# h for the gate turned in blocks of 32 and moved through memory, and the gate computed token tile by token tile behind the whole projection

## The chip, the cores and the metric

The kernel runs on one core of a Trainium2 chip. The time is that of one execution on the device, in microseconds (us). The engines are PE (matrix products and transposes), DVE (elementwise), ACT (elementwise with functions and scales), POOL and SP, which here issues the transfers (SPq in the profile is its queue).

## The reference

Two layers over 256 tokens of width 1024. Each layer has a half-step feed-forward, a token mixing of two attention groups, a second half-step feed-forward and a per-layer embedding; a final normalisation ends it. The change concerns the last step of a layer, and the feed-forward only in how it hands h on.

```python
def rms_norm(x, g):
    y = x * rsqrt(mean(x * x, axis=-1) + EPS)
    return y * g

def hybrid_layer(h, p_i, ...):
    h = h + 0.5 * swiglu(rms_norm(h, ffn1_norm), ...)
    ...                                   # token mixing, added to h
    h = h + 0.5 * swiglu(rms_norm(h, ffn2_norm), ...)
    gate = sigmoid(rms_norm(h, ple_norm) @ w_ple_gate)    # 1024 x 1024
    h = h + gate * (p_i @ w_ple_proj)                     # p_i: 256 x 256
    return h
```

## The kernel before

The tokens are two tiles of 128 (`t` = 0, 1), each on 128 partitions; h stays on chip as `h[:, t, 0:1024]`, and columns are worked in two halves (`f` or `n` = 0, 1) of 512. Products are made to float32 accuracy from two parts of each operand, a high one and the rest: `mm3` is three matmuls (L265 to L267) of 0.23 us each for 512 columns, "a product" below. All weights stream in once, in pieces of 128x1024 (512 KB) that are numbered in the order of use: SP issues the load of `raw` (L157, 7 buffers), ACT copies the high part `wh` (L161), DVE subtracts to get the low part `wl` (L162); eight buffers hold the parts. The gate's weights in layer 0 are pieces 200 to 207 (200 to 203 the first column half), in layer 1 pieces 403 to 410; the two pieces before them are the projection's.

A product needs its left operand turned, with the inner dimension on partitions. `turn_h` (L379) turns a half row of h: four PE transposes of 128x128 (L385) into a bank of PSUM `xt`, four copies on ACT that scale by the norm's gain (L390, `xf`, tag `w2`, two buffers), a copy for the high part on ACT (L392), a subtraction for the low part on DVE (L393). The row's own scale (one over its root mean square) is applied later, as the scale of the sigmoid.

Work that has to be late in an engine's order is put off by a list: `soon(us, f)` puts f on it, and each product adds its modelled length (0.68 for 512 columns) to a count of PE time; what is due then is written out. `flush` writes out everything that is left. Instructions of one engine run in the order in which they are written, apart from small moves by a scheduler; waits are set from data and from buffers.

`lagging` (L423) runs the last products of a feed-forward, with tile 1 three chunks behind tile 0; with the last chunk of a tile comes `residual` (L412), which adds to h and puts `turn_h` on the list for both halves. Then `ple` (L1079) runs column half by column half: for each half four products of the projection (`pv`), then for tile 0 and for tile 1 eight products of the gate (`e`), the sigmoid on ACT (L1109, `se`), two operations on DVE (L1111 `me`, L1112 `h`), the sum of squares of the new h (ACT L354, `junk_ple`), and in layer 0 `turn_h` on the list for the next feed-forward (`xt_e`, `xf_e`, `xe0h`).

Elsewhere (`add` of the class `Gates`, L511) some tiles are already turned without PE: DVE turns blocks of 32x32 in place (L549), SP stores the tile to memory (L551, `m_`) and loads it back in four strided pieces (L556, `ft_`).

Of the kernel before, what the change touches and what calls it, by code (L numbers as in the profile page):

```python
# [17 lines left out]
P = 128  # L18
T = 256
DM = 1024  # L20
# [25 lines left out]
def turned_order(n):  # L46


    import numpy as np

    return np.arange(n).reshape(n // P, 4, 32).transpose(1, 0, 2).reshape(-1)
# [20 lines left out]
def trunk(ctx: ExitStack, tc: tile.TileContext, xT, xr, pT, w, gains, fgain, consts, out):  # L72
# [12 lines left out]
    def bank(name):  # L85
        return ps.tile([P, 512], F32, tag="A", name=name)
# [46 lines left out]
    at = [0]  # L133
    ids = itertools.count()
    newest_load, newest_wh, newest_wl = [None], [None], [None]
    fence = [None, None]

    class Unit:
# [10 lines left out]
        def load(self, q, i):  # L149
            name = f"{self.u}_{q}_{i}_{next(ids)}"  # L150
            if q not in self.parts:
                self.parts[q] = tuple(w_p.tile([P, PIECE], F32R, tag=f"w{e}", name=f"w{e}{name}") for e in "hl")
            n = PIECE // self.sub
            wh, wl = (t[:, i * n : (i + 1) * n] for t in self.parts[q])
            r = raw_p.tile([P, PIECE], F32, tag="raw", name=f"raw{name}")[:, :n]
            a = q * PIECE + i * n
            newest_load[0] = nc.sync.dma_start(r, w[self.u, :, a : a + n])  # L157
            for c in range(self.cut):
                a = slice(c * n // self.cut, (c + 1) * n // self.cut)
                two = (  # L160
                    nc.scalar.activation(wh[:, a], r[:, a], AF.Copy),  # L161
                    nc.vector.tensor_tensor(wl[:, a], r[:, a], wh[:, a].bitcast(F32), ALU.subtract),  # L162
                )
                newest_wh[0], newest_wl[0] = two
                for i, f in zip(two, fence):
                    if f is not None:
                        after(i, f)
# [77 lines left out]
    def soon(us, f):  # L245
        due.append((pe[0] + us, len(due), f))
# [8 lines left out]
    def flush():  # L255
        while due:
            i = min(due)
            due.remove(i)
            i[2]()
# [3 lines left out]
    def mm3(o, a, b, start, stop, **kw):  # L263
        (ah, al), (bh, bl) = a, b
        nc.tensor.matmul(o, ah, bh, start=start, stop=False, **kw)  # L265
        nc.tensor.matmul(o, ah, bl, start=False, stop=False, **kw)  # L266
        newest_mm[0] = nc.tensor.matmul(o, al, bh, start=False, stop=stop, **kw)  # L267
        tick(0.36 if o.shape[-1] <= T else 0.68)

    def both(x, *ix):  # L270
        return tuple(t[ix] for t in x)

    def tok(x, k, t):

        return both(x, slice(None), k, slice(t * P, (t + 1) * P))
# [9 lines left out]
    def wide(us):  # L285

        return lambda k: us[k // 4].at(k % 4, 0, 512)
# [13 lines left out]
    def half(f):  # L301
        return slice(f * 512, (f + 1) * 512)
# [76 lines left out]
    def turn_h(x, t, n, gcol, name):  # L379

        a = bank(f"xt{t}{n}_{name}")
        behind = newest_mm[0]
        for j in range(4):
            c = 4 * n + j
            after(nc.tensor.transpose(a[:, j * P : (j + 1) * P], h[:, t, c * P : (c + 1) * P], ident), behind)  # L385

        f = flat("w2", f"xf{t}{n}_{name}").rearrange("p (a b) -> p a b", a=4)
        for j in range(4):
            c = gcol + 4 * n + j
            nc.scalar.activation(f[:, j], a[:, j * P : (j + 1) * P], AF.Copy, scale=g_sb[:, c : c + 1])  # L390
        xh, xl = both(x, slice(None), slice(4 * n, 4 * n + 4), slice(t * P, (t + 1) * P))
        nc.scalar.activation(xh, f, AF.Copy)  # L392
        nc.vector.tensor_tensor(xl, f, xh.bitcast(F32), ALU.subtract)  # L393

    def column(r, name):

        d = wt("w1", f"col_{name}")
        nc.vector.tensor_tensor(d[:, :, :P], r.rearrange("p (a b) -> p a b", a=2), ident.unsqueeze(1).to_broadcast([P, 2, P]), ALU.mult)
        c = tp.tile([P, 2], F32, tag="col", name=f"c_{name}")
        nc.vector.reduce_sum(c, d[:, :, :P], axis=AX.X)  # L400
        return c
# [7 lines left out]
    def four(name):  # L409
        return [[bank(f"{name}{t}{n}") for n in range(2)] for t in range(2)]  # L410

    def residual(x, n, d, t, scale, tag, gcol, wait=(1.2, 1.9)):  # L412

        for f in range(2):
            c = half(f)
            done = nc.vector.scalar_tensor_tensor(h[:, t, c], d[t][f], scale, h[:, t, c], op0=ALU.mult, op1=ALU.add)
            soon(wait[f], lambda f=f: turn_h(x, t, f, gcol, tag))
        for f in range(2):
            n.add(t, half(f))
        n.done(t)  # L420
        return done

    def lagging(chunks, d, x, scale, tag, gcol, lag, first=True):  # L423

        nx, nn = new_x(f"x_{tag}"), Norm(tag)
        N = len(chunks)
        for i in range(N + lag):
            for t, c in ((0, i), (1, i - lag)):
                if 0 <= c < N:
                    u, j, k = chunks[c]  # L430
                    down_mm(d, u, j, x(k), x.at(k), t, first and c == 0, c == N - 1)
                    if c == N - 1:
                        done = residual(nx, nn, d, t, scale, tag, gcol)
                        if t == 0 and fence[1] is not None:

                            fence[1] = done
        return nx, nn
# [130 lines left out]
    def ffn(x, n, tag, gcol, between=None, feed=None):  # L568
# [163 lines left out]
        nc.vector.tensor_tensor(b, p[5], v, ALU.subtract)  # L732
        to_h(1, 0, v)
        fence[1] = to_h(1, 1, b)
        return lagging(rest, d, gates, 0.5, tag, gcol, 3, False)

    def mix(x, n, L, g0):
        st = {}
# [340 lines left out]
    def ple(x, n, xp, L, gcol):  # L1079
        last = gcol is None  # L1080
        if last:
            nx = None
            fg = f_p.tile([P, DM], F32, tag="f4h", name="fg")
            nc.sync.dma_start(fg, fgain)
            hg = x_p.tile([P, 2, DM], F32, tag="xh", name="hg")
        else:
            nx = new_x(f"xe{L}")
        nn = Norm(f"ple{L}")
        up = Unit(2)
        for f in range(2):  # L1090
            c = half(f)
            wf = wide([Unit(4) for _ in range(2)])
            v = [bank(f"pv{L}{f}{t}") for t in range(2)]
            for k in range(2):
                for t in range(2):
                    mm3(v[t], tok(xp, k, t), up.at(k, c.start, c.stop), k == 0, k == 1, skip_group_check=True)
            for t in range(2):

                step = 256 if last and f == t == 1 else 512
                for a in range(0, 512, step):  # L1100
                    p = slice(a, a + step)
                    hc = h[:, t, c.start + a : c.start + a + step]
                    e = bank(f"e{L}{f}{t}{a}")[:, :step]
                    for k in range(KC):
                        mm3(e, tok(x, k, t), both(wf(k), slice(None), p), k == 0, k == KC - 1, skip_group_check=True)
                    if f == t == 0:
                        flush()
                    s = flat("w0", f"se{L}{f}{t}{a}")[:, :step]
                    sig = nc.scalar.activation(s, e, AF.Sigmoid, scale=n.col(t))  # L1109
                    m = flat("w1", f"me{L}{f}{t}{a}")[:, :step]  # L1110
                    nc.vector.tensor_tensor(m, v[t][:, p], s, ALU.mult)  # L1111
                    nc.vector.tensor_tensor(hc, m, hc, ALU.add)  # L1112
                    nn.add(t, slice(c.start + a, c.start + a + step))
                    if last:
                        nc.vector.tensor_tensor(hg[:, t, c.start + a : c.start + a + step], hc, fg[:, c.start + a : c.start + a + step], ALU.mult)
                    else:
                        soon(4.4 if f == 0 else 2.8, lambda t=t, f=f: turn_h(nx, t, f, gcol, f"e{L}"))
                if f:
                    nn.done(t)
                    if last:  # L1120
                        leave(hg, nn, t)
        if not last:
            table_after(SILU, sig)
        return nx, nn
# [38 lines left out]
def _weights(i):  # L1163
# [9 lines left out]
    for L in range(DEPTH):  # L1173

        def wide(w, m):

            units.extend(cols(w[k : k + 512], m) for k in range(0, DM, 512))
# [49 lines left out]
        ffn("ffn2")  # L1227
        units.append(cols(i["w_ple_proj"][L], ar(DM)))
        for m in range(0, DM, 512):
            wide(i["w_ple_gate"][L], ar(m, m + 512))  # L1230
    return np.stack(units)


def _gains(i):
    import numpy as np

    names = ("ffn1_norm", "mix_norm", "q_lat_norm", "kv_lat_norm", "sb_out_norm", "mla_out_norm", "ffn2_norm", "ple_norm")
    g = [i[n][L].reshape(-1, P) for L in range(DEPTH) for n in names] + [i["final_norm"].reshape(-1, P)]
    return np.ascontiguousarray(np.concatenate(g).T)


# [45 lines left out]
```

## Time and profile before

| what | us |
| --- | --- |
| median of 3 runs | 986.97 (986.43 to 987.26) |
| the profiled execution, its own time | 986.99 |
| its span, first to last instruction | 985.2 |
| PE busy in it | 973.5 (99%) |
| DVE busy | 841.8 (85%) |
| ACT busy | 644.2 (65%) |
| raw weight loads: 338 of 512 KB, from issue to landing, median | 5.5 |

The profile is of one execution. "Busy" counts the time in which an engine runs an instruction. PE rows overlap: a matmul of 0.39 us follows the one before after 0.23. A row of a timeline has the start, the length, the engine, the line and operation, output and inputs, and how many instructions it stands for; in brackets stand the idle time before it and what ended that. The embedding of layer 0 begins with the residual of tile 0 at 458.05, that of layer 1 with the one at 942.89.

### The profile page before, as it was taken

The page shows a single profiled execution, that of the slowest core. Times are in us where ns is not written, and L with a number is a line of the kernel's source. Part 1 is how long each engine was busy: PE and PEld are TensorE (multiplying, and loading weights), DVE is VectorE, ACT ScalarE, POOL GpSimd, SP SyncE. Part 2 cuts the span into 40 slices and gives each one's busy share as a digit, 9 for nine tenths or more (in the row PEclk, how much of TensorE's full clock was granted, in tenths as well). Part 3 has the DMA queues.
Part 4 walks back from the last instruction along what each step waited for, and adds up shares of the span by engine and source line. Part 5 has one row for each costly group of instructions (what it writes and reads, how often), then busy time and mean ns, then how long its engine had stood idle before and what let it go on. Part 6 is the DMA issues. An engine that isn't in the chain of part 4 may idle for free.

```text
span 985.2 us, 13903 instructions
## 1 busy us (share of the span) xinstructions
PE 973.5 (99%) x4880; PEld 823.8 (84%) x4880; DVE 841.8 (85%) x1025; ACT 644.2 (65%) x958; POOL 55.5 (6%) x59
## 2 busy tenths in 40 slices
PE   9999999999999999999999999999999999999997
PEld 7888888899978888888888888889998888888886
DVE  5799899965689998999799989998656999989994
ACT  6756566856587566657776655667757866656663
POOL 0000000200120000001110000003000200000020
PEclk9999999999999999999999999999999999999999
DMA  8948766763074788666648686658602667876651
GB/s 295 365 153 296 244 199 214 255 231 113 11 246 156 250 263 303 177 229 219 230 134 286 229 275 212 215 210 298 206 32 71 229 199 253 294 228 202 222 173 44
DMA packets 85174, 208.39 MB, mean 212 GB/s; under 512 B 13680, under 2 KB 33264, under 8 KB 85104
## 3 DMA queue, kind: packets, MB, share of 16 engines
q1 hardware_dynamic: 84672, 206.93, 62.9%
q8 instruction: 38, 0.62, 0.3%
q10 hardware_dynamic: 432, 0.57, 0.2%
q14 instruction: 32, 0.26, 0.1%
HBM read 195.94 MB, written 11.53 MB: 211 GB/s over the span
## 4 chain that ended last, share of the span: by engine, by line
PE 93%; DVE 3%; ACT 1%; issue 1%; DMA 1%; POOL 0%; POOLq 0%; SPq 0%; DVEq 0%; ACTq 0%
PE p_b L265 4%; PE p_b L267 4%; PE p_b L266 3%; PE g_a L265 3%; PE g_a L267 3%; PE g_a L266 3%; PE g_b L267 3%; PE g_b L266 3%; PE g_b L265 3%; PE p_a L266 3%; PE p_a L267 3%; PE p_a L265 3%; PE d_a L266 3%; PE d_b L265 3%; PE d_a L267 3%; PE d_b L267 3%
## 5 line engine op out<-in xcount | busy, mean ns | idle before, releaser
L162 DVE TENSOR_TENSOR wl<-raw,wh 128x1024 fp32r<-128x1024 f32 (+1 forms) x278 | 321.8, 1190 | 63.3 <-ACT wh L161 60.6
L161 ACT ACTIVATE wh<-raw 128x1024 fp32r<-128x1024 f32 (+1 forms) x278 | 281.6, 1038 | 100.1 <-DMA raw<-in_w 19.1
L202 ACT ACTIVATE wh<-raw 128x1024 fp32r<-128x1024 f32 x133 | 139.8, 1062 | 112.7 <-DVE raw L197 63.1
L203 DVE TENSOR_TENSOR wl<-raw,wh 128x1024 fp32r<-128x1024 f32 x133 | 161.2, 1221 | 10.3 <-ACT wh L202 8.5
L197 DVE TENSOR_TENSOR raw<-raw,raw 128x1024 f32<-128x1024 f32 x76 | 92.6, 1222 | 1.3 <-DMA raw<-in_w 0.8
L265 PE MATMUL d_a<-wh,fh_a 128*128 128x512 f32 x108 | 42.4, 392 | 0.0
L265 PE MATMUL d_b<-wh,fh_b 128*128 128x512 f32 x108 | 42.4, 392 | 0.0
L267 PE MATMUL d_a<-wh,fl_a 128*128 128x512 f32 x108 | 42.1, 389 | 0.0
L267 PE MATMUL d_b<-wh,fl_b 128*128 128x512 f32 x108 | 42.1, 389 | 0.0
L266 PE MATMUL d_b<-wl,fh_b 128*128 128x512 f32 x108 | 42.0, 389 | 0.0
L266 PE MATMUL d_a<-wl,fh_a 128*128 128x512 f32 x108 | 42.0, 389 | 0.0
L265 PE MATMUL g_a<-wh,x0h 128*128 128x512 f32 x80 | 31.3, 393 | 0.7 <-ACT x0h L314 0.7
L267 PE MATMUL g_a<-wh,x0l 128*128 128x512 f32 x80 | 31.0, 389 | 0.0
L266 PE MATMUL g_a<-wl,x0h 128*128 128x512 f32 x80 | 31.0, 389 | 0.0
L265 PE MATMUL g_b<-wh,x_mix0h 128*128 128x512 f32 x64 | 25.1, 392 | 0.0
L265 PE MATMUL g_b<-wh,x_mix1h 128*128 128x512 f32 x64 | 25.1, 392 | 0.0
L265 PE MATMUL g_a<-wh,xe0h 128*128 128x512 f32 x64 | 25.0, 391 | 0.0
L267 PE MATMUL u_a<-wh,x0l 128*128 128x512 f32 x64 | 24.9, 389 | 0.0
L265 PE MATMUL u_a<-wh,x0h 128*128 128x512 f32 x64 | 24.9, 392 | 0.0
L266 PE MATMUL u_a<-wl,x0h 128*128 128x512 f32 x64 | 24.9, 389 | 0.0
L267 PE MATMUL g_b<-wh,x_mix0l 128*128 128x512 f32 x64 | 24.9, 389 | 0.0
L267 PE MATMUL g_b<-wh,x_mix1l 128*128 128x512 f32 x64 | 24.9, 389 | 0.0
(527 smaller groups left out, 2688.5 us busy)
## 6 DMA issues: line engine op xcount, KB each, us to landing
raw<-in_w SPq DMA_DIRECT2D x338, 512.0 KB, 5.5
m_b<-pr_b SPq DMA_DIRECT2D x20, 256.0 KB, 2.5
ft_b<-m_b SPq DMA_DIRECT2D x80, 64.0 KB, 2.9
raw<-in_w SPq DMA_DIRECT2D x16, 256.0 KB, 4.6
m_a<-pr_a SPq DMA_DIRECT2D x16, 256.0 KB, 2.4
ft_a<-m_a SPq DMA_DIRECT2D x64, 64.0 KB, 3.0
xin<-in_xT SPq DMA_DIRECT2D x4, 256.0 KB, 5.0
h<-in_xr SPq DMA_DIRECT2D x2, 512.0 KB, 8.7
```

The source lines that it names most:

```text
L161: nc.scalar.activation(wh[:, a], r[:, a], AF.Copy),
L162: nc.vector.tensor_tensor(wl[:, a], r[:, a], wh[:, a].bitcast(F32), ALU.subtract),
L197: nc.vector.tensor_tensor(self.raw[o], self.raw[a], self.raw[b], op)
L202: newest_wh[0] = nc.scalar.activation(wh, r, AF.Copy)
L203: nc.vector.tensor_tensor(wl, r, wh.bitcast(F32), ALU.subtract)
L265: nc.tensor.matmul(o, ah, bh, start=start, stop=False, **kw)
L266: nc.tensor.matmul(o, ah, bl, start=False, stop=False, **kw)
L267: newest_mm[0] = nc.tensor.matmul(o, al, bh, start=False, stop=stop, **kw)
```

## The change

Between the second feed-forward and the gate, `move_h` takes the place of `turn_h`: DVE turns blocks of 32 (`hb`), SP stores (`mh`) and loads back (`hf`) through memory, ACT scales in place and copies, DVE subtracts. The rows of the gate's weights and the gains of its norm are put in the order that this gives. The lag of the last products is 4 instead of 3. `ple` makes all eight products of the projection first, then goes token tile by token tile and, within one, half by half; the list is flushed as tile 1 begins; loads from then on are kept behind tile 0's last load back; the first feed-forward's `turn_h` for half 0 and half 1 of tile 0 are due after 4.4 us.

```diff
@@ -133,6 +133,7 @@
     at = [0]
     ids = itertools.count()
     newest_load, newest_wh, newest_wl = [None], [None], [None]
+    load_fence, newest_back = [None], [None]
     fence = [None, None]
     class Unit:
@@ -155,6 +156,8 @@
             r = raw_p.tile([P, PIECE], F32, tag="raw", name=f"raw{name}")[:, :n]
             a = q * PIECE + i * n
             newest_load[0] = nc.sync.dma_start(r, w[self.u, :, a : a + n])
+            if load_fence[0] is not None:
+                after(newest_load[0], load_fence[0])
             for c in range(self.cut):
                 a = slice(c * n // self.cut, (c + 1) * n // self.cut)
                 two = (
@@ -392,6 +395,36 @@
         nc.scalar.activation(xh, f, AF.Copy)
         nc.vector.tensor_tensor(xl, f, xh.bitcast(F32), ALU.subtract)
+    def move_h(x, t, n, gcol, name):
+        pr = flat("w1", f"hb{t}{n}_{name}")
+        turned = nc.vector.transpose(pr, h[:, t, half(n)])
+        m = mem_p.tile([P, 4, P], F32, tag="turn", name=f"mh{t}{n}_{name}")
+        nc.sync.dma_start(m, pr.rearrange("p (q r) -> p q r", q=4))
+        a = wt("w2", f"hf{t}{n}_{name}", 4, P)
+        def back():
+            for q in range(4):
+                i = nc.sync.dma_start(a[32 * q : 32 * q + 32], m[:, q].rearrange("(a f) r -> f a r", a=4))
+            if t == 0:
+                newest_back[0] = i
+        def parts():
+            f = a.rearrange("p a (j s) -> p j a s", j=4)
+            c = gcol + 4 * n
+            for j in range(4):
+                nc.scalar.activation(f[:, j], f[:, j], AF.Copy, scale=g_sb[:, c + j : c + j + 1])
+            xh, xl = (in_runs(q) for q in both(x, slice(None), slice(4 * n, 4 * n + 4), slice(t * P, (t + 1) * P)))
+            two = nc.scalar.activation(xh, f, AF.Copy), nc.vector.tensor_tensor(xl, f, xh.bitcast(F32), ALU.subtract)
+            if t == n == 0:
+                fence[:] = two
+        soon(BACK + 0.1 * n, back)
+        soon(PARTS + 0.1 * n, parts)
+        return turned
     def column(r, name):
         d = wt("w1", f"col_{name}")
@@ -409,18 +442,21 @@
     def four(name):
         return [[bank(f"{name}{t}{n}") for n in range(2)] for t in range(2)]
-    def residual(x, n, d, t, scale, tag, gcol, wait=(1.2, 1.9)):
+    def residual(x, n, d, t, scale, tag, gcol, far, wait=(1.2, 1.9)):
         for f in range(2):
             c = half(f)
             done = nc.vector.scalar_tensor_tensor(h[:, t, c], d[t][f], scale, h[:, t, c], op0=ALU.mult, op1=ALU.add)
-            soon(wait[f], lambda f=f: turn_h(x, t, f, gcol, tag))
+            if far:
+                done = move_h(x, t, f, gcol, tag)
+            else:
+                soon(wait[f], lambda f=f: turn_h(x, t, f, gcol, tag))
         for f in range(2):
             n.add(t, half(f))
         n.done(t)
         return done
-    def lagging(chunks, d, x, scale, tag, gcol, lag, first=True):
+    def lagging(chunks, d, x, scale, tag, gcol, lag, first=True, far=False):
         nx, nn = new_x(f"x_{tag}"), Norm(tag)
         N = len(chunks)
@@ -430,7 +466,7 @@
                     u, j, k = chunks[c]
                     down_mm(d, u, j, x(k), x.at(k), t, first and c == 0, c == N - 1)
                     if c == N - 1:
-                        done = residual(nx, nn, d, t, scale, tag, gcol)
+                        done = residual(nx, nn, d, t, scale, tag, gcol, far)
                         if t == 0 and fence[1] is not None:
                             fence[1] = done
@@ -732,7 +768,8 @@
         nc.vector.tensor_tensor(b, p[5], v, ALU.subtract)
         to_h(1, 0, v)
         fence[1] = to_h(1, 1, b)
-        return lagging(rest, d, gates, 0.5, tag, gcol, 3, False)
+        return lagging(rest, d, gates, 0.5, tag, gcol, 3 if between is None else 4, False, between is not None)
     def mix(x, n, L, g0):
         st = {}
@@ -1087,14 +1124,23 @@
             nx = new_x(f"xe{L}")
         nn = Norm(f"ple{L}")
         up = Unit(2)
-        for f in range(2):
-            c = half(f)
-            wf = wide([Unit(4) for _ in range(2)])
-            v = [bank(f"pv{L}{f}{t}") for t in range(2)]
-            for k in range(2):
-                for t in range(2):
-                    mm3(v[t], tok(xp, k, t), up.at(k, c.start, c.stop), k == 0, k == 1, skip_group_check=True)
+        us = [[Unit(4) for _ in range(2)] for f in range(2)]
+        wf = [wide(u) for u in us]
+        up.ready()
+        us[0][0].ready()
+        v = [[bank(f"pv{L}{f}{t}") for t in range(2)] for f in range(2)]
+        for k in range(2):
             for t in range(2):
+                for f in range(2):
+                    mm3(v[f][t], tok(xp, k, t), up.at(k, f * 512, (f + 1) * 512), k == 0, k == 1, skip_group_check=True)
+        for t in range(2):
+            if t:
+                flush()
+            for f in range(2):
+                c = half(f)
+                if f:
+                    load_fence[0] = newest_back[0]
                 step = 256 if last and f == t == 1 else 512
                 for a in range(0, 512, step):
@@ -1102,23 +1148,20 @@
                     hc = h[:, t, c.start + a : c.start + a + step]
                     e = bank(f"e{L}{f}{t}{a}")[:, :step]
                     for k in range(KC):
-                        mm3(e, tok(x, k, t), both(wf(k), slice(None), p), k == 0, k == KC - 1, skip_group_check=True)
-                    if f == t == 0:
-                        flush()
+                        mm3(e, tok(x, k, t), both(wf[f](k), slice(None), p), k == 0, k == KC - 1, skip_group_check=True)
                     s = flat("w0", f"se{L}{f}{t}{a}")[:, :step]
                     sig = nc.scalar.activation(s, e, AF.Sigmoid, scale=n.col(t))
                     m = flat("w1", f"me{L}{f}{t}{a}")[:, :step]
-                    nc.vector.tensor_tensor(m, v[t][:, p], s, ALU.mult)
+                    nc.vector.tensor_tensor(m, v[f][t][:, p], s, ALU.mult)
                     nc.vector.tensor_tensor(hc, m, hc, ALU.add)
                     nn.add(t, slice(c.start + a, c.start + a + step))
                     if last:
                         nc.vector.tensor_tensor(hg[:, t, c.start + a : c.start + a + step], hc, fg[:, c.start + a : c.start + a + step], ALU.mult)
                     else:
-                        soon(4.4 if f == 0 else 2.8, lambda t=t, f=f: turn_h(nx, t, f, gcol, f"e{L}"))
-                if f:
-                    nn.done(t)
-                    if last:
-                        leave(hg, nn, t)
+                        soon(2.8 if f == t == 1 else 4.4, lambda t=t, f=f: turn_h(nx, t, f, gcol, f"e{L}"))
+            nn.done(t)
+            if last:
+                leave(hg, nn, t)
         if not last:
             table_after(SILU, sig)
         return nx, nn
@@ -1227,15 +1270,22 @@
         ffn("ffn2")
         units.append(cols(i["w_ple_proj"][L], ar(DM)))
         for m in range(0, DM, 512):
-            wide(i["w_ple_gate"][L], ar(m, m + 512))
+            wide(i["w_ple_gate"][L][_far()], ar(m, m + 512))
     return np.stack(units)
+def _far():
+    import numpy as np
+    return np.concatenate([k + turned_order(512) for k in range(0, DM, 512)])
 def _gains(i):
     import numpy as np
     names = ("ffn1_norm", "mix_norm", "q_lat_norm", "kv_lat_norm", "sb_out_norm", "mla_out_norm", "ffn2_norm", "ple_norm")
-    g = [i[n][L].reshape(-1, P) for L in range(DEPTH) for n in names] + [i["final_norm"].reshape(-1, P)]
+    g = [i[n][L][_far() if n == "ple_norm" else slice(None)].reshape(-1, P) for L in range(DEPTH) for n in names] + [i["final_norm"].reshape(-1, P)]
     return np.ascontiguousarray(np.concatenate(g).T)
```

In the printed order of instructions a name is followed by numbers: for pieces of weights, `raw_1_0_205_4629` is piece 205; for `hf_b_4419` and its like the number only tells tiles apart. On SP, in layer 0, before:

```order
L157 DMA raw_1_0_203_4571<-in_w 128x1024
L157 DMA raw_0_0_204_4649<-in_w 128x1024
L157 DMA raw_1_0_205_4661<-in_w 128x1024
L157 DMA raw_0_0_206_4685<-in_w 128x1024
L157 DMA raw_1_0_207_4697<-in_w 128x1024
```

and after:

```order
L158 DMA raw_1_0_203_4597<-in_w 128x1024
L404 DMA mh_b_4417<-hb_b_4415 128x512
L404 DMA mh_b_4423<-hb_b_4421 128x512
L409 DMA hf_b_4419<-mh_b_4417 32x4x128 x4
L409 DMA hf_b_4425<-mh_b_4423 32x4x128 x4
L404 DMA mh_b_4467<-hb_b_4465 128x512
L404 DMA mh_b_4473<-hb_b_4471 128x512
L158 DMA raw_0_0_204_4617<-in_w 128x1024
L409 DMA hf_b_4469<-mh_b_4467 32x4x128 x4
L409 DMA hf_b_4475<-mh_b_4473 32x4x128 x4
L158 DMA raw_1_0_205_4629<-in_w 128x1024
L158 DMA raw_0_0_206_4641<-in_w 128x1024
```

Twenty transfers of h stand in the row of the weights' loads now, all sixteen loads back ahead of pieces 205 to 207 (4419 and 4425 are tile 0's halves, 4469 and 4475 tile 1's, in the same two buffers). In layer 1 the first load behind them is piece 407, the first of the second column half.

On ACT, in layer 0, around the first sigmoid, before:

```order
L390 ACTIVATE xf_b_4501<-xt_b_4496,g_sb 128x128 x4
L390 ACTIVATE xf_b_4522<-xt_b_4517,g_sb 128x128
L392 ACTIVATE x_b0h<-xf_b_4501 128x4x128
L390 ACTIVATE xf_b_4522<-xt_b_4517,g_sb 128x128 x3
L161 ACTIVATE wh_1_0_205_4659<-raw_1_0_205_4661 128x1024
L392 ACTIVATE x_b0h<-xf_b_4522 128x4x128
L1109 ACTIVATE se_4581<-e_4532,hr_b_4389 128x512
L161 ACTIVATE wh_0_0_206_4683<-raw_0_0_206_4685 128x1024
```

and after:

```order
L164 ACTIVATE wh_0_0_204_4615<-raw_0_0_204_4617 128x1024
L1153 ACTIVATE se_4607<-e_4558,hr_b_4389 128x512
L418 ACTIVATE hf_b_4469<-hf_b_4469,g_sb 128x4x32 x4
L357 ACTIVATE junk_ple_00_4612,hss_ple_4484<-h 128x512
L420 ACTIVATE x_b0h<-hf_b_4469 128x4x128
L418 ACTIVATE hf_b_4475<-hf_b_4475,g_sb 128x4x32 x4
L420 ACTIVATE x_b0h<-hf_b_4475 128x4x128
L164 ACTIVATE wh_1_0_205_4627<-raw_1_0_205_4629 128x1024
```

Tile 1's parts of x and the copy of piece 205 stood ahead of the first sigmoid; they stand behind it now, the copy last.

On PE, in layer 0, around the transposes `xt_e` for the next feed-forward, before (4646 is the gate's second half, tile 0):

```order
L267 MATMUL e_4646<-wh_0_0_204_4647,x_b0l 128x512
L265 MATMUL e_4646<-wh_1_0_205_4659,x_b0h 128x512
L266 MATMUL e_4646<-wl_1_0_205_4660,x_b0h 128x512
L267 MATMUL e_4646<-wh_1_0_205_4659,x_b0l 128x512
L385 MATMUL xt_e_4668<-c_sb,h 128x128 x4
L265 MATMUL e_4646<-wh_1_0_205_4659,x_b0h 128x512
```

and after (4614 is the second half of tile 0, 4696 the first half of tile 1):

```order
L270 MATMUL e_4614<-wh_1_0_207_4651,x_b0l 128x512
L388 MATMUL xt_e_4660<-c_sb,h 128x128 x4
L268 MATMUL e_4614<-wh_1_0_207_4651,x_b0h 128x512
L269 MATMUL e_4614<-wl_1_0_207_4652,x_b0h 128x512
L270 MATMUL e_4614<-wh_1_0_207_4651,x_b0l 128x512
L388 MATMUL xt_e_4684<-c_sb,h 128x128 x4
L268 MATMUL e_4696<-wh_0_0_200_4498,x_b0h 128x512
```

`xt_e_4684` turns the half of h that 4614 itself changes; it stands right behind 4614's last matmul.

In layer 1, PE goes from the gate's first half of tile 0 (9195) to the second (9252) so:

```order
L270 MATMUL e_9195<-wh_1_0_406_9232,x_b1l 128x512
L268 MATMUL e_9252<-wh_0_0_407_9253,x_b1h 128x512
L268 MATMUL e_9315<-wh_0_0_403_9135,x_b1h 128x512
L269 MATMUL e_9252<-wl_0_0_407_9254,x_b1h 128x512
L270 MATMUL e_9252<-wh_0_0_407_9253,x_b1l 128x512
```

The scheduler has put one matmul of tile 1 (9315) between two of 9252.

## The prediction

> **What bounds the kernel now.** The top of the profile comes first: span, busy shares, and the chain of work that ended last.
>
> ```profile
> span 985.2 us, 13903 instructions
> PE 973.5 (99%) x4880; PEld 823.8 (84%) x4880; DVE 841.8 (85%) x1025; ACT 644.2 (65%) x958; POOL 55.5 (6%) x59
> PE 93%; DVE 3%; ACT 1%; issue 1%; DMA 1%; POOL 0%; POOLq 0%; SPq 0%; DVEq 0%; ACTq 0%
> ```
>
> PE carries the time: 973.5 of 985.2 us busy, 93% of the chain. So a removed PE instruction is worth its whole duration, and a wait of PE costs its whole length. The view of PE's waits (what it waited for: us, times, longest) says how few there are:
>
> ```profile
> PE warm L107 <- POOL neg_half L103: 1.0, 1, 1.0
> PE wo L267 <- DVE y1l L315: 0.9, 1, 0.9
> PE xt_e L385 <- DVE h L1112: 0.2, 1, 0.2
> ```
>
> No wait is longer than 1.0 us, and around the per-layer embedding the only one is 0.2 us. Everything there (loads, splits, sigmoid) is covered by PE work. The question is therefore what the change takes off PE, and which cover it breaks.
>
> **The transposes removed.** After the second feed-forward, four groups of four PE transposes a layer go: eight groups, these 32 instructions of the grouped view, with PE's timeline around two of them (start, us, engine, line):
>
> ```profile
> L385 PE MATMUL xt_b<-c_sb,h 128*128 128x128 f32 x32 | 4.8, 272 | 0.0
> 458.06 0.39 PE L265 MATMUL d_b<-wh,fh_b 128*128 128x512 f32 x1
> 458.74 0.39 PE L265 MATMUL d_b<-wh,fh_b 128*128 128x512 f32 x1
> 459.43 0.60 PE L385 MATMUL xt_b<-c_sb,h 128*128 128x128 f32 x4
> 460.56 0.60 PE L385 MATMUL xt_b<-c_sb,h 128*128 128x128 f32 x4
> ```
>
> One product (three matmuls) starts every 0.68 us (458.06 to 458.74). From one group of transposes to the next, with one product between, are 1.13 us, so a group costs 0.45. Removed: 8 x 0.45 = **-3.6 us**. No other PE work appears or goes: products, weights and splits keep their number.
>
> **What replaces them, and its queue.** Each half row of h now takes a DVE block transpose, one DMA to memory, four back, four scalings and a copy on ACT, a subtraction on DVE. The kernel moves tiles this way elsewhere, so it has rows for nearly every step:
>
> ```profile
> 458.05 1.29 DVE L416 SCALAR_TENSOR_TENSOR h<-d_b,h 128x512 f32<-128x512 f32 x2
> 313.70 1.30 DVE L549 STREAM_TRANSPOSE pr_b<-pr_b 128x512 f32<-128x512 f32 x2
> 459.25 4.63 DVE L162 TENSOR_TENSOR wl<-raw,wh 128x1024 fp32r<-128x1024 f32 x4
> 463.79 0.69 DVE L393 TENSOR_TENSOR x_b0l<-xf_b,x_b0h 128x512 fp32r<-128x512 f32 x1
> 377.97 0.92 SPq L551 DMA_DIRECT2D m_b<-pr_b  x2
> 380.06 3.65 SPq L556 DMA_DIRECT2D ft_b<-m_b  x8
> L556 SPq DMA_DIRECT2D ft_b<-m_b x96: 302/423/669, 317.8 to 900.0; - x96
> ...
> DMA to landing us min/median/max: 1.7/2.9/5.6
> 446.11 5.78 ACT L161 ACTIVATE wh<-raw 128x1024 fp32r<-128x1024 f32 x6
> 478.93 1.14 ACT L390 ACTIVATE xf_e<-xt_e,g_sb 128x128 f32<-128x128 f32 x4
> 480.52 0.65 ACT L392 ACTIVATE xe0h<-xf_e 128x512 fp32r<-128x512 f32 x1
> ```
>
> I count from R, the start of the residual of token tile 0. Tile 0: residual to R+1.29, two block transposes to 2.5. The first store issues at 1.9; store to load-back is 2.09 (377.97 to 380.06), so the eight loads back issue from 4.0 to 7.65 (0.455 each). The first half's four are issued by 5.85 and land at 7.6 to 7.8 with the shortest landing (1.7); at 2.9 they land about a microsecond later. Then four scalings 1.14, copy 0.65, subtraction 0.69: the first half's parts exist at R+10.4. The second half's ACT work stands behind two weight copies (0.96 each, 5.78/6), so its subtraction ends near R+14.0.
>
> In the new order tile 1's loads back write the two buffers that tile 0's occupy, so SP holds the first four until the subtraction of half 0 (10.4) and the next four until that of half 1 (14.0): R+14.0 to 15.8. Queued on SP behind them are the raw weights of the second column half: 205, 206, 207 in layer 0, and 407 to 410 in layer 1. Before, they stood in a row behind 203 or 406 with no such wait. **The first late load issues at R+15.8.**
>
> PE meanwhile: tile 1's last product ends at R+5.4 (lag 4 gives PE the same sequence as 3, since four chunks are left), eight products for the projection (8 x 0.68 = 5.44) reach 10.9, and eight of the gate's tile 0, half 0 reach **T = R+16.3**. Its first half of x (10.4) is just in time; its second is needed, low part first missing, near 14.1 and exists at 14.0: I take 0, with up to 1.5 if landings are at the median. The four extra products of projection moved ahead are what pays for the trip; without them PE would wait another 2.7.
>
> **The weights that come late.** They land at the earliest 3.0 after issue:
>
> ```profile
> L157 SPq DMA_DIRECT2D raw<-in_w x278: 327/328/1347, 1.2 to 947.6; - x139
> ...
> DMA to landing us min/median/max: 3.0/5.5/10.4
> 473.30 0.39 PE L267 MATMUL e<-wh,x_b0l 128*128 128x512 f32 x1
> 473.78 0.69 ACT L1109 ACTIVATE se<-e,hr_b 128x512 f32<-128x512 f32 x1 [2.15 <-PE e L267]
> 475.23 0.69 DVE L1112 TENSOR_TENSOR h<-me,h 128x512 f32<-128x512 f32 x1
> 476.05 0.61 ACT L354 ACTIVATE junk_ple<-h 128x512 bf16<-128x512 f32 x1
> ```
>
> So 407 is there at T+2.5 (median T+5.0). But ACT can't take it then: ahead of its copy stand the sigmoid, tile 1's first scalings, the sum of squares `junk_ple` (it waits for the new h), and tile 1's remaining parts. A product's last matmul starting at 473.30 lets the next start at 473.53; h is finished at 475.92, so T+2.4. Sum of squares to T+3.05, copy of half 0 to 3.7, scalings 4.85, copy 5.5, weight copy to about T+6.4, its subtraction (4.63/4 = 1.16; 1.2 beside other work) to **T+7.65**. The second matmul of a product needs the low part. In layer 1 the piece is the first of the half, its second matmul normally at T+0.23: **+7.4**. In layer 0 piece 204 was loaded ahead of the held DMAs and gives two products (1.36): the second matmul of 205 is due at T+1.59: **+6.1**. The pieces after it follow at 1.1 to 1.2 us each on ACT and DVE, under PE's 1.36, so they add nothing. Nor do the later halves: tile 1 uses the same weights, 10.9 us in which SP gets ahead again.
>
> **The transposes moved in layer 0.** Pending work is now flushed when tile 1 begins, so the transposes of tile 0, half 1 stand right behind that half's last product and wait for its sigmoid, product, and addition:
>
> ```profile
> 478.29 0.60 PE L385 MATMUL xt_e<-c_sb,h 128*128 128x128 f32 x4
> 481.89 0.69 DVE L1112 TENSOR_TENSOR h<-me,h 128x512 f32<-128x512 f32 x1
> 497.81 0.66 PE L385 MATMUL xt_e<-c_sb,h 128*128 128x128 f32 x4 [0.24 <-DVE h L1112]
> ```
>
> Before has the same arrangement on ACT and DVE (a group of transposes at 478.29, a last product, then that product's epilogue with the earlier group's x parts in between): h ends at 482.58, 4.29 after 478.29. PE is through with the group and the product after 1.13, so it waits 4.29 + 0.05 - 1.13 = **+3.2**. The cover it had, a whole next set of products, is gone. The 0.24 at 497.81 belongs to the last group, whose delay stays.
>
> **The clock.** Before has no idle PE inside the run long enough to touch it, only its ends show:
>
> ```profile
> 977.59 0.28 PE L267 MATMUL e<-wh,x_b1l 128*128 128x256 f32 x1
> 980.00:980.50 0.50, 0.00 (x0) 0.00 (x0) 0.00 (x0) 0.00 (x0) 0.34 (x2) 1.00 0.00 0
> 980.50:981.00 0.50, 0.00 (x0) 0.00 (x0) 0.00 (x0) 0.00 (x0) 0.50 (x1) 0.79 0.00 0
> 981.00:981.50 0.50, 0.00 (x0) 0.00 (x0) 0.45 (x1) 0.45 (x1) 0.02 (x1) 0.50 0.07 16
> L107 PE MATMUL warm<-ones x22: 275/421/582, 1.0 to 5.1; 128*128 128x128 f32 x22
> L374 PE MATMUL rw_a<-dg_a,ones x8: 272/275/275, 189.6 to 675.3; 128*128 128x128 f32 x8
> ```
>
> The eleventh figure of the windows (after the five busy columns) is the granted clock: PE ends at 977.87, the clock is 1.00 until 980.5, 0.79 in the next half microsecond, then 0.50. Idle for about 2.9 us therefore halves it. At the start the same matmul shape takes a median of 421 ns against 275 later, from 1.0 to about 4.5: 3.5 us at half pace, in which 1.75 us of work is lost. The gaps of 6.1 and 7.4 are both beyond 2.9: 2 x 1.75 = **+3.5** (bounds: 0 if it stays full, 5.3 if the 3.2 us gap halves it as well; two is nearest to the row, the third sits at its edge).
>
> The Trainium skill, "TensorE: Matmul & The Clock Gate", section "Part 1: The HAM clock gate (the "warmup" mystery)", says that the clock depends on activity over a free-running window of about 3.4 us and that the first such stretch of new work runs at half. By its window, a gap of 6 or 7 us always holds the drop; 3.2 us needn't. Returning after 1 to 2 windows would cost 1.7 to 3.4 each, an estimate by that page: 3.4 to 6.8 in place of 3.5. The trace's 2.9 us is shorter than its window, its 3.5 us of slow start agrees.
>
> **Sum:** -3.6 + 6.1 + 7.4 + 3.2 + 3.5 = +16.6. The profiled execution took 986.99 us (span plus 1.8), the median of the runs is 986.97, so one may stand for the other: **1003.5 us**. Bounds kept for the range: late loads at their median landing, +0.5 to +1.5 on each; x parts +1.5.
>
> **Rivals.**
> - *The clock stays full* (gaps broken up by stray matmuls, one of which the order puts inside the layer 1 gap): 1003.5 - 3.5 = **1000.0**.
> - *A third drop, longer returns*: +1.75 and up to +3 more: **1007**.
> - *Landing alone binds, ACT serves the late weight first in effect*: issue R+15.8, landing 3.0, copy 1.06, subtraction 1.2 end at R+21.1; needed at 16.55 (layer 1) and 17.9 (layer 0): 4.6 + 3.2 + 3.2 - 3.6 = +7.4, no clock drop of the third gap: **994.4**, up to 998 with drops. Against it: the copies stand behind the sums of squares in program order.
> - *Not slower: the loads come in time.* It decides whether the first held load issues 3.0 + 1.06 + 1.2 = 5.3 us before T, at R+11.0; my chain gives 15.8. Only a trip whose second half ends by R+9 would do it, and the scalings, copies and subtractions of the two halves alone take 2 x 2.48 after the first landing at 7.6. Then -3.6 + 3.2 = -0.4: **986.6**; if the epilogue in layer 0 were covered too, 983.4.
>
> **How the numbers follow.** Forecast 0.60 (own range 1000 to 1007), full clock 0.20, third drop 0.07, landing alone 0.07, loads in time 0.06. A measurement of this kernel tells about 0.2%, 2 us, from no change: the first four are slower (0.94), the last is split evenly, 0.03 within 0.2% and 0.03 faster. Range: 996 to 1008, leaving out the loads in time, most of the landing case and the longest drops.
>
> **What the profile of after would show.** PE's waits: about 6 to 7.5 us once in each layer for a `wl` or `wh` of the gate's second half, and 3 us for h at the transposes in layer 0. SP's waits: two new ones a layer at the loads back, for the x parts. The raw load of 205 and 407 issued 15 to 16 us after R. Granted clock at 0.50 behind those gaps. 32 fewer transposes. Wrong if tile 1's loads back issue before R+10, if the first late load issues by R+11, or if PE goes from tile 0's first half to its second within 1 us.

## The result

The changed kernel takes 1009.62 us (1009.23 to 1010.36) against 986.86 for the kernel before: a ratio of 1.023 (1.0217 to 1.0243), slower. The forecast was 1003.5, in a range of 996 to 1008. The profiled execution took 1009.91, its span is 1008.1 against 985.2, so 22.9 us are to be placed. The top of its page:

```profile
span 1008.1 us, 13924 instructions
PE 979.0 (97%) x4848; PEld 826.1 (82%) x4848; DVE 847.5 (84%) x1033; ACT 646.4 (64%) x958; POOL 41.9 (4%) x59
PE 90%; DVE 4%; ACT 3%; issue 2%; DMA 1%; POOL 0%; POOLq 0%; DVEq 0%; ACTq 0%
```

PE has 32 instructions fewer (4848 against 4880), as it should, and yet is busy for 5.5 us longer; the granted clock below shows why. Its waits (what was waited for: us, times, longest):

```profile
PE e L268 <- ACT wh L164: 11.3, 2, 6.3
PE xt_e L388 <- DVE h L1156: 5.5, 2, 3.0
PE q L269 <- DVE x_a1l L396: 0.9, 2, 0.6
```

The third line lies in layer 1's token mixing, and the kernel before has no such line. Where the others lie, from PE's timeline (the bracket has the idle time and its releaser): the first three rows are the last matmul on piece 204 and the first two on piece 205 of layer 0, the next two the transposes of tile 0's and of tile 1's second half, the last three the end of piece 406 and the start of piece 407 in layer 1:

```profile
475.64 0.39 PE L270 MATMUL e<-wh,x_b0l 128*128 128x512 f32 x1
481.00 0.79 PE L268 MATMUL e<-wh,x_b0h 128*128 128x512 f32 x1 [4.98 <-ACT wh L164]
482.26 0.80 PE L269 MATMUL e<-wl,x_b0h 128*128 128x512 f32 x1 [0.47 <-DVE wl L165]
491.09 0.66 PE L388 MATMUL xt_e<-c_sb,h 128*128 128x128 f32 x4 [3.04 <-DVE h L1156]
512.47 1.11 PE L388 MATMUL xt_e<-c_sb,h 128*128 128x128 f32 x4 [2.50 <-DVE h L1156]
974.24 0.39 PE L270 MATMUL e<-wh,x_b1l 128*128 128x512 f32 x1
980.97 1.22 PE L268 MATMUL e<-wh,x_b1h 128*128 128x512 f32 x2 [6.34 <-ACT wh L164]
982.23 0.80 PE L269 MATMUL e<-wl,x_b1h 128*128 128x512 f32 x1
```

The bracket counts idle time from the modelled end of the row before, which is 0.39 long where the next row starts after 0.23. What a wait costs is therefore better read from the starts, as the prediction counted it. The second matmul on piece 205 needs the weight's low part (L269); it was due two steps of 0.23 after 475.64, at 476.10, and started 6.2 later. That on piece 407 was due three steps after 974.24 (the matmul of tile 1 lies between), at 974.92, and started 7.3 later. The transposes behind the flush were due at 487.89, 0.23 after the matmul at 487.66, and were 3.2 late; the last ones were due at 509.81, after the matmul at 509.58, and were 2.7 late, against 0.4 in the kernel before.

In or behind each of the four waits the clock halves. In windows of 0.1 us its changes lie at 478.00, 484.83, 491.65, 495.06, 512.15, 515.55, 979.75 and 986.57: to 0.02, all lie whole multiples of 3.413 apart. Windows on that grid (length, busy time of PE, PEld, which is its weight loads, DVE, ACT and POOL, then the granted clock, the DMA share and GB/s):

```profile
474.59:478.00 3.41, 1.44 (x7) 0.86 (x5) 1.38 (x2) 2.92 (x8) 0.00 (x0) 1.00 0.91 249
478.00:481.41 3.41, 0.41 (x1) 0.29 (x1) 1.81 (x3) 3.38 (x8) 0.00 (x0) 0.50 0.98 332
481.41:484.83 3.42, 2.96 (x7) 2.09 (x7) 3.16 (x3) 1.54 (x2) 0.00 (x0) 0.50 1.01 398
488.24:491.65 3.41, 0.56 (x5) 0.56 (x6) 1.89 (x3) 1.97 (x6) 0.00 (x0) 1.00 0.39 156
491.65:495.06 3.41, 3.41 (x10) 2.64 (x10) 0.69 (x1) 2.65 (x8) 0.86 (x2) 0.50 0.02 5
508.74:512.15 3.41, 1.23 (x6) 0.69 (x4) 3.41 (x5) 0.00 (x0) 0.00 (x0) 1.00 0.73 294
512.15:515.55 3.40, 3.08 (x10) 2.60 (x11) 2.83 (x6) 2.65 (x8) 1.28 (x2) 0.50 0.26 75
972.93:976.34 3.41, 1.70 (x8) 1.08 (x6) 0.86 (x2) 1.61 (x5) 0.00 (x0) 1.00 0.68 158
976.34:979.75 3.41, 0.00 (x0) 0.00 (x0) 1.92 (x3) 3.06 (x9) 0.00 (x0) 1.00 0.98 368
979.75:983.16 3.41, 2.15 (x4) 1.34 (x5) 2.90 (x3) 3.41 (x5) 0.00 (x0) 0.50 0.41 166
983.16:986.57 3.41, 3.41 (x9) 2.67 (x8) 2.42 (x3) 0.60 (x1) 0.00 (x0) 0.50 0.00 0
```

PE worked at half pace from 481.0 to 484.83 (with 0.47 idle), 491.65 to 495.06, 512.47 to 515.55 and 980.97 to 986.57: 3.4, 3.4, 3.1 and 5.6 us, of which half is lost, 7.7 in all. Of this, 1.0 ran before the two second matmuls, while PE would have waited for a low part anyway. What lies behind the late starts (482.26, 491.65, 512.47 and 982.23) counts 1.3, 1.7, 1.5 and 2.2, in all 6.7.

The account of the 22.9, then: transposes -3.6, piece 205 6.2, piece 407 7.3, behind the flush 3.2, at the last transposes 2.7 less the 0.4 of before, clock 6.7, sum 22.1. Layer 1 gives 0.9 more between the first residual of its first feed-forward and the first of its token mixing (661.73 to 767.73 before, 676.07 to 782.98 after), and the two waits for the low part of x there, 0.9 in all, are as large; why that part comes late was not traced. With it the sum is 23.0, so nothing of size is left unplaced.

On SP and ACT the chain is as the prediction has it:

```profile
468.60 5.09 SPq L409 DMA_DIRECT2D hf_b<-mh_b  x8
473.73 11.43 SPq L158 DMA_DIRECT2D raw<-in_w  x10
474.76 0.69 ACT L1153 ACTIVATE se<-e,hr_b 128x512 f32<-128x512 f32 x1 [2.13 <-PE e L270]
478.08 1.26 ACT L418 ACTIVATE hf_b<-hf_b,g_sb 128x128 f32<-128x128 f32 x4
479.38 0.63 ACT L420 ACTIVATE x_b0h<-hf_b 128x512 fp32r<-128x512 f32 x1
479.91 1.99 ACT L164 ACTIVATE wh<-raw 128x1024 fp32r<-128x1024 f32 x2
```

The residual of tile 0 starts at 458.18, the load of piece 205 issues 15.55 later, and its copy on ACT follows tile 1's parts of x without a gap.

### The profile page after: what moved, and what is told of

The parts are those of the page before. It is cut to its first block, busy times and chain, and to the rows that moved or that the text cites. A ratio compares the mean times of both kernels' runs of the same rounds, so it can differ in the third digit from the quotient of the medians.

```text
span 1008.1 us, 13924 instructions
## 1 busy us (share of the span) xinstructions
PE 979.0 (97%) x4848; PEld 826.1 (82%) x4848; DVE 847.5 (84%) x1033; ACT 646.4 (64%) x958; POOL 41.9 (4%) x59
## 4 chain that ended last, share of the span: by engine, by line
PE 90%; DVE 4%; ACT 3%; issue 2%; DMA 1%; POOL 0%; POOLq 0%; DVEq 0%; ACTq 0%
PE p_b L268 3%; PE p_b L270 3%; PE p_b L269 3%; PE g_a L268 3%; PE g_a L270 3%; PE g_a L269 3%; PE g_b L270 3%; PE g_b L268 3%; PE g_b L269 3%; PE p_a L268 3%; PE p_a L269 3%; PE p_a L270 3%; PE d_b L270 3%; PE d_b L269 3%; PE d_b L268 3%; PE u_a L269 3%
## 5 line engine op out<-in xcount | busy, mean ns | idle before, releaser
L269 PE MATMUL d_a<-wl,fh_a 128*128 128x512 f32 x108 | 42.0, 389 | 0.0
L269 PE MATMUL d_b<-wl,fh_b 128*128 128x512 f32 x108 | 42.0, 389 | 0.0
L269 PE MATMUL g_a<-wl,x0h 128*128 128x512 f32 x80 | 31.1, 391 | 0.0
L270 PE MATMUL g_a<-wh,xe0l 128*128 128x512 f32 x64 | 25.5, 399 | 0.0
L269 PE MATMUL g_a<-wl,xe0h 128*128 128x512 f32 x64 | 25.2, 394 | 0.0
```

## Experiments

The kernel before was run beside each; its median there was 987.0 to 987.1. Edits are to the changed kernel unless said.

**Which of two things makes the weight late: SP or ACT.** Tile 1's loads back get memory that is free at that time, so that they wait for no subtraction.

```diff
-        a = wt("w2", f"hf{t}{n}_{name}", 4, P)
+        a = wt("w2", ...) if t == 0 else f_p.tile([P, 4, P], F32, tag=F_TAGS[n], ...)
```

> Tile 1's loads back get buffers of their own, so SP no longer holds them for tile 0's subtractions; order of every engine unchanged. If the order on ACT binds (the copies of pieces 205 and 407 stand behind tile 1's parts of x and the sum of squares), the late loads issue some 2 us earlier, the two waits of PE for wh stay at 5.0 and 6.3 us, and the time stays at 1009.6, give or take 1. If the late issue of the loads binds, both waits shrink by about 2 us, and the time falls to about 1005.

1009.15 (1007.82 to 1011.27). The loads issue 1.7 us earlier, PE waits as long as it did:

```profile
PE e L268 <- ACT wh L164: 11.3, 2, 6.3
472.04 12.95 SPq L158 DMA_DIRECT2D raw<-in_w  x10
480.07 2.93 ACT L164 ACTIVATE wh<-raw 128x1024 fp32r<-128x1024 f32 x3
```

ACT's order binds; the hold on SP alone is worth nothing here.

**The flush.**

```diff
         for t in range(2):
-            if t:
-                flush()
```

> The list is not flushed as tile 1 begins, so the transposes of tile 0, half 1 come 4.4 us of products after that half's last product. If the 3.0 us wait of PE there is the epilogue's latency and the clock's drop of 1.7 us follows from it, both go: 1009.6 - 4.7 = 1004.9 (1003.5 to 1006.5, since a drop elsewhere can move). If the wait only moves to another product, the time stays within 1 us of 1009.6.

1004.01 (1001.76 to 1004.83), 5.6 less. The wait of 3.0 is gone, the last one is not:

```profile
PE xt_e L388 <- DVE h L1154: 2.0, 1, 2.0
```

**The clock's part.** Small matmuls of constants, into a bank of PSUM that is free at that time, fill the four waits.

```diff
+    def stray(o, n):
+        for _ in range(n):
+            i = nc.tensor.matmul(o[:, :P], ones, ones, start=True, stop=True, ...)
+            after(i, newest_mm[0])
+            newest_mm[0] = i
```

> The four waits stay, but PE runs small matmuls of constants in them (46 before piece 205, 27 and 21 before the two groups of transposes that wait, 60 before piece 407), a little shorter than each wait. If the clock's drops cost what I count from the slowed stretches (2.0 + 1.7 + 1.4 + 2.9 = 8.0), the clock stays at 1.00 and the time is about 1001.6 (1000.5 to 1004). If the slowed stretches are hidden behind something else, the time stays at 1009.6.

1017.95 (1017.92 to 1018.05): a miss of sizing. The clock stayed full (0.998), but each call took 0.227 us (46 calls in 10.43), twice what I had counted, so the calls outlasted the waits:

```profile
475.99 10.43 PE L384 MATMUL idle<-ones 128*128 128x128 f32 x92
```

> As the run before with stray matmuls, but sized by what it showed: one call of 128x128 float32 took 0.226 us of PE, twice what I had counted, so 20, 12, 9 and 26 calls fill 4.5, 2.7, 2.0 and 5.9 us of the four waits. If the clock's drops cost 8.0, the clock stays at 1.00 and the time is about 1001.6 (1000.5 to 1003.5). If the slowed stretches are hidden behind something else, it stays at 1009.6.

1002.49 (1001.82 to 1002.98), 7.1 less than with the change alone, with the granted clock at 0.999. PE now runs them up to the end of the waits:

```profile
476.08 4.63 PE L384 MATMUL idle<-ones 128*128 128x128 f32 x40
481.22 0.50 PE L268 MATMUL e<-wh,x_b0h 128*128 128x512 f32 x1 [0.51 <-ACT wh L164]
970.11 5.97 PE L384 MATMUL idle<-ones 128*128 128x128 f32 x52
976.62 0.73 PE L268 MATMUL e<-wh,x_b1h 128*128 128x512 f32 x2 [0.54 <-ACT wh L164]
```

The weights come no earlier, and the time falls by about what the slow stretches count (6.7 behind the late starts, 7.7 whole). So the clock's drops cost about 7, not the 3.5 forecast.

**Loads first, own buffers, no flush.** Pieces up to 205 (layer 0) and 408 (layer 1) are loaded and split ahead of h's transfers.

```diff
         us[0][0].ready()
+        us[0][1].ready()
+        us[1][0].ready()
```

> Three edits together: own buffers for tile 1's loads back, pieces up to 205 (layer 0) and 408 (layer 1) loaded ahead of h's transfers, no flush. If the waits and the clock's drops behind them are the whole loss, what is left is the removed transposes, -3.6: about 983.4 (982.5 to 985.5). If the way through memory costs something of its own (transfers that slow the loads, the later half of x), the time is 987 or more.

998.76 (998.0 to 1003.77): the long waits are gone, but not the loss. On DVE six subtractions of weights now stood ahead of tile 0's parts of x, and PE waited in the gate's first half instead; in layer 0 the granted clock fell to 0.50 twice, at about 473.1 and 486.8.

```profile
465.80 6.86 DVE L165 TENSOR_TENSOR wl<-raw,wh 128x1024 fp32r<-128x1024 f32 x6
472.58 1.28 DVE L420 TENSOR_TENSOR x_b0l<-hf_b,x_b0h 128x512 fp32r<-128x512 f32 x2
473.31 0.79 PE L270 MATMUL e<-wh,x_b0l 128*128 128x512 f32 x1 [1.23 <-DVE x_b0l L420]
```

**Each part alone.** First h through memory, with the embedding in its former order (the loop of the kernel before in `ple`):

> One part alone: h moved through memory, the embedding in its former order (half by half, no early projection of the second half). The four products of projection that covered the trip are gone, so I expect PE to wait for x in the gate's first product (about 1.8 us), at its fifth (1.6) and in tile 1's first (2) in each layer, and no long wait for a weight: 986.9 - 3.6 + 2 x 5.4 = 994 (990 to 998 with or without drops of the clock). If the trip is what is costly whatever the order, 1003 or more; if the new order alone is what costs, below 988.

1001.43 (1000.52 to 1002.43): worse than expected, and mostly not by the waits for x that I had named (1.4 in each layer).

```profile
PE e L268 <- ACT wh L164: 8.5, 2, 4.6
468.02 1.28 ACT L418 ACTIVATE hf_b<-hf_b,g_sb 128x128 f32<-128x128 f32 x4 [2.79 <-DMA hf_b<-mh_b]
469.86 1.99 ACT L164 ACTIVATE wh<-raw 128x1024 fp32r<-128x1024 f32 x2
470.95 0.80 PE L268 MATMUL e<-wh,x_b0h 128*128 128x512 f32 x1 [4.56 <-ACT wh L164]
```

ACT waits for the first half of h to land, and behind that stand the copies of the gate's own first pieces, whose loads stand ahead of h's transfers on SP. It is the same form of loss as in the whole change, a tile early in ACT's row that comes late, at another piece.

Then the new order alone: `turn_h` as before, the former rows of the weights, lag 3, no fence on the loads.

> The other part alone: h turned on PE as before, the embedding in the new order with its flush. No transfer of h stands in the loads' row, so the weights come in time, and what is left is the wait behind the flush (3.0) with its clock drop (1.7): 986.9 + 4.7 = 991.6 (990 to 993). If the weights are late by the order of the halves itself, two waits of some us for wh show and the time is 997 or more.

996.77 (995.34 to 996.99), 5 more than expected. No weight is late, but both waits for h are there:

```profile
PE xt_e L388 <- DVE h L1153: 5.5, 2, 3.0
501.19 1.23 DVE L200 TENSOR_TENSOR raw<-raw,raw 128x1024 f32<-128x1024 f32 x1 [2.50 <-DMA raw<-in_w]
502.93 0.68 DVE L1152 TENSOR_TENSOR me<-pv,se 128x512 f32<-128x512 f32 x1
504.67 0.68 DVE L1153 TENSOR_TENSOR h<-me,h 128x512 f32<-128x512 f32 x1
505.41 1.12 PE L388 MATMUL xt_e<-c_sb,h 128*128 128x128 f32 x4 [2.44 <-DVE h L1153]
```

So the fourth wait belongs to the order and not to h's trip. DVE stands for 2.5 us at a sum of raw weights of the next feed-forward, whose load is late; the last `me` and h stand behind it. The test of that: no flush, and the sum kept behind the last addition to h (`last_h`) on DVE. In the whole change with only the flush taken out, this wait stayed at 2.0 (above), so it takes the moved sum to remove it.

```diff
-            nc.vector.tensor_tensor(self.raw[o], self.raw[a], self.raw[b], op)
+            i = nc.vector.tensor_tensor(self.raw[o], self.raw[a], self.raw[b], op)
+            if last_h[0] is not None:
+                after(i, last_h[0])
```

> The new order alone, without the flush, and with the sums of the next feed-forward's weights kept behind the last addition to h on DVE. Theory now: the fourth wait (2.4 us at the last transposes of h, also in the run with the order alone) comes from DVE, where a sum of raw weights that wait for their load stands ahead of the addition to h. Then both waits and their clock drops go and the order by itself costs nothing: 987 (986 to 988.5). Rival: the late loads themselves hold PE, the wait moves to the first product that needs those weights, and the time is 989.5 or more.

987.94 (987.62 to 988.53), a ratio of 1.0009 (1.0 to 1.0018) to the kernel before, without a wait for h or a weight in the embedding. The order by itself is harmless once these two waits are out.

**The change mended.** Loads of all eight pieces ahead of tile 1's loads back, their splits where they were first needed, own buffers, tile 1's parts 6 us later, no flush.

> All of the change, mended: tile 1's loads back in buffers of their own; the eight pieces of the gate loaded ahead of tile 1's loads back, their splits left where they were first needed but those of the second half kept behind tile 0's parts of x; tile 1's parts of x due 6 us later; no flush. In the order all six copies of pieces 202 to 207 stand ahead of the first sigmoid. If the four waits and the clock are the whole loss, what is left is -3.6: 983.4, with up to 2 more for the second half of x (983 to 985.5). If something else in the way through memory costs time, 987 or more.

992.26 (991.45 to 993.15). The wait of the largest size is now 1.3, for tile 1's parts of x in layer 1; I had put them too late. With that, the place of three loads and the sums mended:

> The mended change of the run before, with its own small waits addressed: pieces 205 to 207 load behind tile 0's loads back instead of between, tile 1's parts of x ahead of the second sigmoid (in layer 1 the copy stood behind it), and the sums behind the addition to h. The run before lost 2.6 us at four waits for x in layer 1, 1 in layer 0, 2 in the mixing behind it. If those are gone, 992.3 - 4 = 988 (986.5 to 990); if its remaining loss is from transfers that slow each other, it stays at 991 or more. It beats the kernel before only if all of the 5.5 are gone (below 986.5), which I give 1 in 5.

989.75 (988.2 to 990.5), 1.0025 (1.0015 to 1.0034). Of its span (988.1, 2.9 over before), layer 1's embedding takes 42.5 against 42.3 of before, so the removed transposes are spent there on two waits of 0.7; what is left is in the mixing of layer 1:

```profile
PE v L275 <- ACT x_a1h L402: 1.4, 1, 1.4
PE e L276 <- DVE wl L170: 1.4, 2, 0.7
PE q L276 <- DVE x_a1l L403: 1.2, 1, 1.2
```

No version was found that beats the kernel before. Whether these last waits can be ordered away was not tried.

## Why the prediction was wrong

The sign was right, and so were the removed transposes, the two late weights and the wait behind the flush, in place, mechanism and size. The time was 6.1 too low, 1.6 above the range. Two terms of the sum failed: the last transposes of h, put at nothing, cost 2.3, and the clock's drops, of which two were priced, were four, 3.2 more than forecast. With the 0.9 in layer 1's mixing, where the prediction has no term, these make 6.4; the span went 6.3 beyond the sum.

- *Transposes, -3.6.* As forecast: 32 fewer.
- *Late weights, +6.1 and +7.4.* By the starts they measured 6.2 and 7.3. The chain on ACT was right and alone decisive (own buffers changed nothing). The weight copy started 5.4 after the gate's first half (forecast 5.5), and PE's second matmul on the piece, the one with the low part, was the last to be held, as forecast. The rival in which landing alone binds is refuted by the run with own buffers.
- *Behind the flush, +3.2.* 3.2; without the flush it is gone.
- *The last transposes, 0.* This step failed: "the 0.24 at 497.81 belongs to the last group, whose delay stays". That idle time became 2.50. The same holds for "10.9 us in which SP gets ahead again". In the new order, tile 1 uses each of the gate's eight pieces a second time, 10.9 us of products later, and eight is the number of buffers. The next feed-forward's copies wait for PE to give one free:

```profile
494.32 1.06 ACT L164 ACTIVATE wh<-raw 128x1024 fp32r<-128x1024 f32 x1 [0.73 <-PE e L270]
496.12 1.07 ACT L164 ACTIVATE wh<-raw 128x1024 fp32r<-128x1024 f32 x1 [0.74 <-PE e L270]
498.48 5.30 SPq L197 DMA_DIRECT2D raw<-in_w  x4
508.25 1.23 DVE L200 TENSOR_TENSOR raw<-raw,raw 128x1024 f32<-128x1024 f32 x1 [2.56 <-DMA raw<-in_w]
```

  In the order alone, the loads of the next feed-forward's summed weights issue from 491.55 on, before from 483.74. Part of these 7.8 us is the flush's own wait: in the run without it they issue from 488.78 on, 5.0 late. That the buffers' longer use makes them late is read from these rows; a ninth buffer was not tried. That the sum on DVE carries the lateness to h is shown by the run that moved it.
- *The clock, +3.5.* This term was mis-sized: 6.7 by the trace, 7.1 by the run that filled the waits. I priced two drops of 1.75. Behind the late weights they cost 1.3 and 2.2; that these add up to 3.5 is partly luck. The one in layer 1 spanned 5.6 us of work, since a first window that was idle for a third didn't bring the clock back. The other two drops were not in the sum: the 3.0 of the flush and the unforeseen 2.5 were enough, and cost 1.7 and 1.5. Even the bound of 5.3 was too low, since it had three drops. The flush's gap was left out because idle time of about 2.9 us had halved the clock at the end of the kernel before; the windows show that the length of the gap alone does not decide, but how much of it falls into one step of the grid. The Trainium skill, "TensorE: Matmul & The Clock Gate", section "Part 1: The HAM clock gate (the "warmup" mystery)", speaks of a free-running window of 3413 ns, and the trace agrees, since every change lies on a grid of 3.41. An estimate by its windows, up to 3.4 per drop, stood beside the forecast and not in the range. Where it asks for a window without work, the trace differs: 2.0 us of idle within one window were enough. The prediction's "a gap of 6 or 7 us always holds the drop" does not follow from such a window either: on a grid of 3.41 only a gap of 6.8 always holds a whole step. The gap at piece 205 held none without PE work (1.44 and 0.41 us in the two steps that it touched), and the clock dropped all the same.

## What to carry to other kernels

When a step leaves the busiest engine for a longer way, count it in the row of every engine that it joins: here the loads, copies and subtractions of weights stood behind a tile that was still on its way, and each of the two late weights cost more than the transposes that were saved. When loops are interchanged, count how long each buffer of the operands stays in use, and who is next in line for it. A wait of 2.5 or 3 us on PE cost itself and, where the clock fell, 1.5 to 1.7 us more.

## What the runs showed of the hardware

- The eight changes of the clock listed above lie on one grid of 3.41 us. By the windows above it fell after one with PE busy for 0 to 1.44 of 3.41 and stayed after one with 1.70; it rose after 2.96 to 3.41 and stayed low after 0.41 and 2.15. So whether a wait costs clock depends on where it falls: the same 3.0 us wait behind the flush dropped it in the changed kernel, while the run with the order alone shows one drop only, at its second wait. On the grid that this drop (504.9) and its return (508.3) give, the two windows that share its first wait hold 1.63 and 2.16 us of busy PE, and the one just ahead of the drop holds 1.47.
- A 128x128 float32 matmul of constants took 0.227 us of PE per call and stands as two instructions in the profile (46 calls: 92 rows, 10.43 us).
